# A first modulation whose bias comes by channels, with three weight tiles on a second queue

## The chip, the cores and the metric

The kernel runs on one core of one Trainium2 chip. The metric is the device time of one execution in microseconds; the kernel before takes 1773.36 us (median of 3 runs). TensorE multiplies matrices, VectorE (DVE in the profile), ScalarE (ACT) and GpSimd (POOL) work on vectors, and SyncE (SP) issues the transfers between the chip's main memory and the core's on-chip memory. Sixteen DMA engines carry them.

## The reference, cut to what matters

One layer of a diffusion backbone over 512 latent tokens and 256 context tokens, 1024 channels wide. Two condition vectors (for the latent and for the context tokens) give six modulation vectors each, by one product with `w_mod` (1024 x 6144) and a bias `b_mod`. The first two of the six shift and scale the first norm:

```python
cond, cond_c = silu(c), silu(c_ctx)
mod = cond @ w_mod + b_mod            # six vectors of 1024; mod_c likewise
h = rmsnorm(x, norm1) * (1 + mod[1]) + mod[0]
cols = h @ w_in                       # input projection, feeds three mixers
...                                   # convolution, recurrence, grid attention, merge, residual
...                                   # second norm, router, 16 experts, residual
```

Everything after the first norm needs `mod[0]` and `mod[1]`; the other four vectors are needed later.

## The kernel before

The program is written out by hand in the order in which it shall run, and each engine takes its instructions in that order. It has a start, a first sub-layer (to about 760 us in the trace), the output projection with the router, and sixteen experts whose weights, 384 chunks of 1 MiB, pass through a ring of buffers; a chunk is loaded when the products with an older one have freed its buffer.

The start does two things side by side. *Tokens*: `load_x` loads each tile of 128 tokens as two pieces of 128 x 512 (2 KB a row, 256 KB a piece, tiles named `y`); `stats` (L248, ScalarE) sums their squares, `scales` (L252 to L257) normalises them, TensorE transposes them (L266), and VectorE and ScalarE copy the transposes to `xT` (L268). *First modulation*: the condition vectors `cc` are put through silu into `cs`; the columns 0 to 2047 of `w_mod` come as eight tiles `wm0[k]` of 128 x 2048 (1 MiB each, k0 to k7, in the buffers A, A, C and wm, two tiles in each), and `mod_mm` (L303) multiplies each with `cs` as four products of 512 columns in four groups of 32 rows, summed over k in one PSUM bank. TensorE has the transposes ahead of these products in its order.

Afterwards the bias is added (`mod_rows`, L307), four transposes bring the rows to channels on partitions (`mod_cols`, L313), a copy takes the two columns that matter out of PSUM (L315), and L368 makes the scale `ga1`. From then on `modulate` (L381, L382) gives the projection's operands, while casts (L353) and differences (L354) split the first projection weights `W` into two parts.

The bias of the rows is read from main memory by `bias_row`: its source pattern is four rows of 512 numbers, each read 32 times, into 128 x 512.

```python
SP.dma_start(out=t, in_=bass.AP(tensor=a["b_mod"].tensor, offset=a["b_mod"].offset + g * 2048,
                                ap=[[512, 4], [0, 32], [1, 512]]))
```

It is called three times: for the first modulation and, later, for the two other groups of columns, whose weights are loaded in slabs (L468). All transfers are issued by SP in the order of the program: `cc`, eight token pieces, the small operands `vecs` (39 columns), k0 to k5, the bias rows, k6, k7, the first two items of the projection's weights, the context tokens.

## Time and profile before

| | us |
|---|---|
| time, median of 3 runs | 1773.36 (1773.16 to 1774.51) |
| profiled execution, first to last instruction | 1770.6 |
| of it, until the first group of projection products ends | 54.3 |
| of it, the first sub-layer after that, to the output projection | 54.3 to 760 |
| of it, experts' products and weights at full rate | 838 to 1770.6 |

Of the profiled execution the profile has the span alone, which begins with the first instruction and ends with the last; the times of the runs also hold what lies around it, so the median stands 2.8 us above the span. Over the span TensorE is busy for 94%, VectorE 32%, ScalarE 21%. Such shares are averages over stages with different limits, and what a change in the first 40 us is worth has to be read from that stage.

### The profile page before, as it was taken

The page shows a single profiled execution, that of the slowest core. Times are in us where ns is not written, and L with a number is a line of the kernel's source. Part 1 is how long each engine was busy: PE and PEld are TensorE (multiplying, and loading weights), DVE is VectorE, ACT ScalarE, POOL GpSimd, SP SyncE. Part 2 cuts the span into 40 slices and gives each one's busy share as a digit, 9 for nine tenths or more (in the row PEclk, how much of TensorE's full clock was granted, in tenths as well). Part 3 has the DMA queues.
Part 4 walks back from the last instruction along what each step waited for, and adds up shares of the span by engine and source line. Part 5 has one row for each costly group of instructions (what it writes and reads, how often), then busy time and mean ns, then how long its engine had stood idle before and what let it go on. Part 6 is the DMA issues. An engine that isn't in the chain of part 4 may idle for free.

```text
span 1770.6 us, 20476 instructions
## 1 busy us (share of the span) xinstructions
PE 1667.7 (94%) x8382; PEld 949.9 (54%) x8382; DVE 572.1 (32%) x1135; ACT 367.7 (21%) x759; POOL 79.0 (4%) x150
## 2 busy tenths in 40 slices
PE   4999999999999999999999999998998998989988
PEld 2767888777777888896343343342432422424322
DVE  3518776435553443334011211121121121202111
ACT  4414445333334332223000010000000100000000
POOL 0214330000000000000000000000000000000000
PEclk8999999999999999999999999999999999999999
DMA  9860111111111233366999999999999999999997
GB/s 343 283 227 25 50 51 67 48 66 66 66 60 42 92 132 109 137 233 238 401 420 420 420 420 421 420 421 420 420 420 421 420 420 421 420 420 420 421 420 299
DMA packets 131690, 487.77 MB, mean 275 GB/s; under 512 B 8973, under 2 KB 12557, under 8 KB 125709
## 3 DMA queue, kind: packets, MB, share of 16 engines
q1 hardware_dynamic: 131596, 486.47, 69.2%
q8 instruction: 66, 1.08, 0.2%
q14 instruction: 28, 0.22, 0.0%
HBM read 484.34 MB, written 2.10 MB: 275 GB/s over the span
## 4 chain that ended last, share of the span: by engine, by line
PE 73%; DMA 11%; DVE 5%; ACT 1%; issue 1%; SPq 0%; DVEq 0%; ACTq 0%
PE pj L1343 19%; PE pj L440 19%; PE acc L1368 9%; PE hg L1397 5%; PE pj L985 4%; PE hg L1311 3%; PE pj L1175 2%; DMA B<-in_w_down_dram 2%; DMA D<-in_w_down_dram 2%; DMA W<-in_w_up_dram 2%; DMA B<-in_w_up_dram 2%; PE acc L910 2%; DVE acc L1400 2%; PE hg L879 1%; DMA A<-in_w_down_dram 1%; PE tp L896 1%
## 5 line engine op out<-in xcount | busy, mean ns | idle before, releaser
L440 PE MATMUL pj<-A,W 128*128 128x512 f32 x1536 | 400.8, 402 | 2.9 <-ACT W L353 1.9
L440 PEld LDWEIGHTS pj<-A,W 128*128 128x128 f32 x1536 | 276.4, 190 | 73.6 <-issue 20.1
L354 DVE TENSOR_TENSOR W<-W 128x512 fp32r<-128x512 f32 (+1 forms) x184 | 121.4, 686 | 155.4 <-ACT W L353 155.2
L1350 DVE TENSOR_TENSOR s<-s,pj 128x512 f32<-128x512 f32 x32 | 22.0, 688 | 453.7 <-PE pj L1343 367.0
L1343 PE MATMUL pj<-W,xe 128*64 128x512 f32 x688 | 156.5, 599 | 7.8 <-DMA W<-in_w_up_dram 4.4
L1348 ACT ACTIVATE s<-pj 128x512 f32<-128x512 f32 x32 | 19.1, 597 | 567.8 <-PE pj L1343 567.8
L1343 PE MATMUL pj<-A,xe 128*64 128x512 f32 x512 | 118.0, 605 | 5.2 <-DMA A<-in_w_gate_dram 4.2
L1397 PE MATMUL hg<-ye,oht 64*128 64x512 f32 x240 | 100.4, 683 | 16.5 <-DVE acc L1400 16.5
L1343 PEld LDWEIGHTS pj<-W,xe 128*64 128x64 f32 x688 | 47.4, 138 | 110.5 <-issue 86.4
L1343 PE MATMUL pj<-B,xe 128*64 128x512 f32 x432 | 98.5, 596 | 6.6 <-DMA B<-in_w_up_dram 4.4
L353 ACT CAST W<-W 128x512 fp32r<-128x512 f32 (+1 forms) x184 | 103.3, 600 | 0.0
L1400 DVE TENSOR_TENSOR acc<-acc,hg 128x512 f32<-128x512 f32 x120 | 77.7, 684 | 37.1 <-PE hg L1397 37.1
L1343 PEld LDWEIGHTS pj<-A,xe 128*64 128x64 f32 x512 | 35.2, 139 | 81.8 <-issue 66.3
L1397 PEld LDWEIGHTS hg<-ye,oht 64*128 64x128 f32 x240 | 32.7, 193 | 81.8 <-DVE acc L1400 69.6
L1389 DVE TENSOR_TENSOR ye<-mod,acc 64x512 f32<-64x512 f32 x30 | 20.6, 686 | 172.2 <-PE acc L1368 171.7
L1368 PE MATMUL acc<-W,at 128*64 128x512 f32 x320 | 71.7, 595 | 2.1 <-DMA W<-in_w_down_dram 2.1
L1343 PEld LDWEIGHTS pj<-B,xe 128*64 128x64 f32 x432 | 29.5, 137 | 70.0 <-issue 52.9
L1358 ACT COPY at<-tp 128x512 f32<-128x512 f32 x32 | 18.8, 586 | 219.1 <-PE tp L1356 218.6
L440 PEld LDWEIGHTS pj<-C,W 128*128 128x128 f32 x384 | 59.2, 190 | 9.2 <-ACT y L612 0.8
L440 PE MATMUL pj<-C,W 128*128 128x256 f32 x384 | 61.8, 283 | 0.0
L1311 PEld LDWEIGHTS hg<-ot,xn 128*128 128x128 f32 x512 | 57.9, 192 | 2.7 <-issue 2.7
L1311 PE MATMUL hg<-ot,xn 128*128 128x128 f32 x512 | 59.1, 276 | 0.2 <-DVE ot L1297 0.2
(289 smaller groups left out, 1875.1 us busy)
## 6 DMA issues: line engine op xcount, KB each, us to landing
W<-in_w_gate_dram SPq DMA_DIRECT2D x44, 1024.0 KB, 18.1
W<-in_w_up_dram SPq DMA_DIRECT2D x42, 1024.0 KB, 17.7
W<-in_w_down_dram SPq DMA_DIRECT2D x40, 1024.0 KB, 18.0
W<-in_w_in_dram SPq DMA_DIRECT2D x34, 1024.0 KB, 4.8
A<-in_w_gate_dram SPq DMA_DIRECT2D x34, 1024.0 KB, 18.1
B<-in_w_up_dram SPq DMA_DIRECT2D x34, 1024.0 KB, 17.5
B<-in_w_down_dram SPq DMA_DIRECT2D x31, 1024.0 KB, 18.1
A<-in_w_up_dram SPq DMA_DIRECT2D x30, 1024.0 KB, 17.9
```

The costliest lines, as they stand in the source:

```text
L353: S.copy(hi[:, sl], raws[n][:, sl])
L354: V.tensor_tensor(lo[:, sl], raws[n][:, sl], hi[:, sl].bitcast(F32), op=ALU.subtract)
L440: PE.matmul(dst, w[wi][:, k, 128 * b:128 * b + 128], src[xi][:, k], start=(k == 0 and p == 0), stop=(k == KT - 1 and p == 2))
L910: PE.matmul(po[r, 128 * cb:128 * cb + 128], vs[c][:, hc], pT[:, 128 * c:128 * c + 128], start=(c == 0), stop=(c == 3))
L985: PE.matmul(st["p"], wb[wi][:, 4 * br + k], yv[br][k][xi], start=(k == 0 and p == 0), stop=(k == 3 and p == 2))
L1175: PE.matmul(st["p"][:, 256 * u:256 * u + 256], mm[k][mi][:, ts], w[wi][:, k], start=(k == 0 and p == 0), stop=(k == KT - 1 and p == 2))
L1311: PE.matmul(px[:, 128 * k:128 * k + 128], xn[:, i, 128 * kk:128 * kk + 128], ot[:, 128 * i:128 * i + 128], start=(i == 0), stop=(i == 3))
L1343: PE.matmul(pg[64 * u:64 * u + 64], xp[:, kk, 64 * (e % 2):64 * (e % 2) + 64], wt[:, k, 512 * u:512 * u + 512], start=(kk == 0), stop=(kk ...
L1350: V.tensor_tensor(est["s", j], est["s", j], pg, op=ALU.mult)
L1368: PE.matmul(est["y"][64 * u:64 * u + 64], lhs, wt[:, k, 512 * u:512 * u + 512], start=(kk == 0), stop=(kk == 15))
L1397: PE.matmul(pc, oht[64 * u:64 * u + 64, 128 * i:128 * i + 128], ye[64 * u:64 * u + 64], start=True, stop=True)
L1400: V.tensor_tensor(av, av, pc, op=ALU.add)
```

## The change

The bias of the first modulation is not loaded as rows any more. Its 2048 numbers stand in sixteen more columns of `vecs`, by channels, and are added in the operation that copies the transposed columns out of PSUM. The PSUM bank with the products' sums is copied by two engines, one half of the columns each. The first three weight tiles are issued by ScalarE's queue, in the program ahead of the tokens; the other five follow the tokens and `vecs` on SP's queue. The other two bias rows stay as they were.

```diff
     out["vecs"] = np.concatenate([kt(a["norm1"][0]), kt(a["norm2"][0]), lb, a["hg_norm"][0][:, None],
                                   np.tile(a["na_q_norm"][0], 2)[:, None], np.tile(a["na_k_norm"][0], 2)[:, None],
-                                  cw], axis=1)
+                                  cw, kt(a["b_mod"][0][0:1024]), kt(a["b_mod"][0][1024:2048])], axis=1)
...
     cc = small([128, KT, 2], "cc")
-    SP.dma_start(out=cc, in_=a["cc"])
-    for i in range(4):
-        load_x(i)
-    vecs = small([128, 39], "vecs")
-    SP.dma_start(out=vecs, in_=a["vecs"])
+    vecs = small([128, 55], "vecs")
...
-    def load_mod0(k):
+    def load_mod0(k, eng):
...
-        SP.dma_start(out=wm, in_=a["w_mod"][k * 128:(k + 1) * 128, 0:2048])
+        eng.dma_start(out=wm, in_=a["w_mod"][k * 128:(k + 1) * 128, 0:2048])
...
     wmt = []
-    for k in range(8):
-        if k == 6:
-            brow0 = bias_row(0)
-        load_mod0(k)
+    SP.dma_start(out=cc, in_=a["cc"])
+    for k in range(3):
+        load_mod0(k, S)
+    for i in range(4):
+        load_x(i)
+    SP.dma_start(out=vecs, in_=a["vecs"])
+    for k in range(3, 8):
+        load_mod0(k, SP)
...
-    def mod_cols(g, mr):
+    def mod_cols(g, mr, bias=None):
...
-        V.tensor_copy(mt, pt.rearrange("p (i j x) -> p j i x", i=4, j=4)[:, :, :, 0:2])
+        pv = pt.rearrange("p (i j x) -> p j i x", i=4, j=4)[:, :, :, 0:2]
+        if bias is None:
+            V.tensor_copy(mt, pv)
+        else:
+            V.tensor_tensor(mt, pv, bias.rearrange("p (j i) -> p j i", j=4).unsqueeze(3).broadcast_to([128, 4, 4, 2]),
+                            op=ALU.add)
...
-    mod0 = mod_cols(0, mod_rows(pm, brow0))
+    mr0 = g512()
+    V.tensor_copy(mr0[:, 0:256], pm[:, 0:256])
+    S.copy(mr0[:, 256:512], pm[:, 256:512])
+    mod0 = mod_cols(0, mr0, vecs[:, 39:55])
```

The line numbers move by a few: L303 stays, L307 and L315 become L372 and L319 for the first modulation, L338 becomes L343.

The start of SP's queue before. A name in brackets is the counter for which a transfer waits; there are eight of them, given out in turn, so that a transfer waits for the one eight places ahead of it.

```order
L190 DMA cc<-in_cc_dram 128x16
L187 DMA y<-in_x_dram 128x512 x7
L187 DMA y<-in_x_dram 128x512 [waits DMAHW0_49]
L194 DMA vecs<-in_vecs_dram 128x39 [waits DMAHW1_49]
L215 DMA A<-in_w_mod_dram 128x2048 [waits DMAHW2_49]
L215 DMA A<-in_w_mod_dram 128x2048 [waits DMAHW3_49]
...
L215 DMA C<-in_w_mod_dram 128x2048 [waits DMAHW7_49]
L203 DMA g<-in_b_mod_dram 128x1x512 [waits DMAHW0_49]
L215 DMA wm<-in_w_mod_dram 128x2048 [waits DMAHW1_49]
L215 DMA wm<-in_w_mod_dram 128x2048 [waits DMAHW2_49]
L338 DMA W<-in_w_in_dram 128x2048 [waits DMAHW3_49]
```

The same place of the change:

```order
L215 DMA cc<-in_cc_dram 128x16
L187 DMA y<-in_x_dram 128x512 x5
L187 DMA y<-in_x_dram 128x512 [waits DMAHW0_49]
L187 DMA y<-in_x_dram 128x512 [waits DMAHW1_49]
L187 DMA y<-in_x_dram 128x512 [waits DMAHW2_49]
L220 DMA vecs<-in_vecs_dram 128x55 [waits DMAHW4_49]
L211 DMA A<-in_w_mod_dram 128x2048 [waits DMAHW5_49]
L211 DMA C<-in_w_mod_dram 128x2048 [waits DMAHW6_49]
L211 DMA C<-in_w_mod_dram 128x2048 [waits DMAHW7_49]
L211 DMA wm<-in_w_mod_dram 128x2048 [waits DMAHW0_49]
L211 DMA wm<-in_w_mod_dram 128x2048 [waits DMAHW1_49]
L343 DMA W<-in_w_in_dram 128x2048 [waits DMAHW2_49]
```

The bias rows and three weight tiles are gone from this queue, and the last three token pieces have waits of their own; DMAHW0 there belongs to the first weight tile on ScalarE's queue.

The start of ScalarE's instructions before (squares of the tokens are `g,ssq<-y`):

```order
L229 ACT_TABLE_LOAD
L229 ACTIVATE csg<-cc 128x16 [waits DMAHW0_49]
L248 ACTIVATE g,ssq<-y 128x512 [waits DMAHW1_49]
L248 ACTIVATE g,ssq<-y 128x512 [waits DMAHW2_49]
L248 ACTIVATE g,ssq<-y 128x512 [waits DMAHW3_49]
```

The same place of the change:

```order
L211 DMA A<-in_w_mod_dram 128x2048 x2
L211 DMA A<-in_w_mod_dram 128x2048 [waits DMAHW3_49]
L229 ACT_TABLE_LOAD
L229 ACTIVATE csg<-cc 128x16 [waits DMAHW1_49]
L248 ACTIVATE g,ssq<-y 128x512 [waits DMAHW2_49]
L248 ACTIVATE g,ssq<-y 128x512
L248 ACTIVATE g,ssq<-y 128x512 [waits DMAHW4_49]
```

Three transfers now stand ahead of the table load, and the third of them waits for DMAHW3, the counter of the second token piece.

## Rows read from the trace of the kernel before

**Rows 1.** Head of the page, and packets of all transfers (counts under a size are cumulative).

```profile
span 1770.6 us, 20476 instructions
...
DMA packets 131690, 487.77 MB, mean 275 GB/s; under 512 B 8973, under 2 KB 12557, under 8 KB 125709
```

**Rows 2.** Stretches: busy time by engine, granted clock, DMA engines' share, rate.

```profile
core 0: us, PE busy (x) PEld busy (x) DVE busy (x) ACT busy (x) POOL busy (x), PEclk, DMA share, GB/s
4.00:10.00 6.00, 0.00 (x0) 0.00 (x0) 0.00 (x0) 4.31 (x13) 0.00 (x0) 1.00 0.93 308
14.00:25.00 11.00, 10.29 (x72) 5.86 (x72) 6.23 (x18) 3.84 (x6) 0.00 (x0) 1.00 1.02 427
25.00:29.50 4.50, 1.06 (x8) 0.16 (x8) 0.00 (x0) 0.00 (x0) 0.00 (x0) 0.82 1.02 268
29.50:36.00 6.50, 3.49 (x16) 0.40 (x16) 0.00 (x0) 0.00 (x0) 0.00 (x0) 0.50 1.01 421
54.33:760.00 705.67, 694.76 (x3752) 552.26 (x3752) 354.75 (x719) 256.80 (x540) 71.21 (x139) 1.00 0.27 93
64.00:67.50 3.50, 3.50 (x32) 3.50 (x31) 0.45 (x2) 1.95 (x4) 0.39 (x1) 1.00 1.04 235
838.00:1770.60 932.60, 868.89 (x3955) 317.04 (x3954) 159.63 (x292) 60.51 (x109) 0.00 (x0) 0.99 1.01 413
```

**Rows 3.** Timeline of TensorE: start, us, then what, with the idle time before.

```profile
14.02 5.86 PE L266 MATMUL pj<-ident,y 128*128 128x128 f32 x32 [14.02 <-DVE y L257]
19.80 3.64 PE L303 MATMUL acc<-A,g 128*32 128x512 f32 x32
23.26 1.04 PE L303 MATMUL acc<-C,g 128*32 128x512 f32 x8
25.42 1.06 PE L303 MATMUL acc<-C,g 128*32 128x512 f32 x8 [1.11 <-DMA C<-in_w_mod_dram]
31.98 1.94 PE L303 MATMUL acc<-wm,g 128*32 128x512 f32 x8 [5.50 <-DMA wm<-in_w_mod_dram]
34.45 1.94 PE L303 MATMUL acc<-wm,g 128*32 128x512 f32 x8 [0.53 <-DMA wm<-in_w_mod_dram]
37.20 1.12 PE L313 MATMUL tp<-ident,g 128*128 128x128 f32 x4 [0.81 <-DVE g L307]
...
102.77 0.60 PE L313 MATMUL tp<-ident,g 128*128 128x128 f32 x4
```

**Rows 4.** Timeline of VectorE around the first modulation's end.

```profile
36.45 0.69 DVE L307 TENSOR_TENSOR g<-acc,g 128x512 f32<-128x512 f32 x1 [13.46 <-PE acc L303]
38.35 0.19 DVE L315 COPY modT<-tp 128x32 f32<-128x32 f32 x1 [1.21 <-PE tp L313]
38.58 0.17 DVE L368 SCALAR_TENSOR_TENSOR ga<-modT,vecs 128x16 f32<-128x16 f32 x1
```

**Rows 5.** Timeline of ScalarE: table load, last squares, first cast of weights.

```profile
0.73 1.28 ACT L229 ACT_TABLE_LOAD   x1 [0.73 <-PEq L1464]
...
10.31 0.63 ACT L248 ACTIVATE g<-y 128x512 f32<-128x512 f32 x1
10.85 0.19 ACT L248 ACTIVATION_READ_ACCUMULATOR g<-y 128x1 f32 x1
...
39.56 0.60 ACT L353 CAST W<-W 128x512 fp32r<-128x512 f32 x1
```

**Rows 6.** Waits of SP's queue, 0 to 50 and 54 to 75 us.

```profile
SPq L187 <- DMA g<-in_b_mod_dram: 4.0, 1, 4.0
...
SPq L468 <- DMA g<-in_b_mod_dram: 4.2, 1, 4.2
```

**Rows 7.** Waits of TensorE, 54 to 760 us: total, times, longest.

```profile
PE hg L711 <- DVE g L712: 4.7, 3, 3.1
PE pj L529 <- DVE W L354: 2.0, 1, 2.0
```

**Rows 8.** Groups by form, 0 to 300 us: copies out of PSUM.

```profile
L268 DVE COPY g<-pj 128x512 f32<-128x512 f32 x4 | 2.8, 691 | 0.7 <-PE pj L266 0.7
L757 DVE COPY g<-hg 128x128 f32<-128x128 f32 x6 | 1.7, 290 | 2.4 <-PE hg L754 2.4
L613 ACT ACTIVATE g<-pj 128x256 f32<-128x256 f32 x8 | 3.0, 379 | 1.4 <-PE pj L440 1.4
```

## The prediction

> **What bounds the kernel now.** I read the span and the packet counts first [rows 1], then stretches of the span with the granted clock and the DMA rate [rows 2], then the timelines of TensorE, VectorE and ScalarE over the first 40 us [rows 3 to 5], and last who waits for whom [rows 6, 7]. After 54 us the kernel is a long train: TensorE is busy in 694.76 of the 705.67 us up to 760, with the DMA engines at 0.27 [rows 2], and what it waits for there is VectorE, 4.7 us the longest item, with no transfer in the list [rows 7]. From 838 us the expert weights stream at 413 GB/s with the engines at 1.01 of their time [rows 2]; each of those loads is issued when a product frees its buffer, so this stream starts when the train before it arrives. Nothing in either part has a clock of its own. I therefore take a shift of the first part's end as a shift of the kernel's end, one for one.

> The first part is where TensorE stands still. The transposes of the normalised tokens run from 14.02, and at 19.80 the products with the first modulation's eight weight tiles (k0 to k7) begin [rows 3]. Four need 3.64 us and k4 follows at once, but k5 waits for its tile until 25.42, k6 until 31.98 and k7 until 34.45 [rows 3]. The last product ends at 36.39, and the evacuation, four transposes and two small operations carry it to 38.75 [rows 3, 4]. So the weights set the end of this part, and the tokens, ready at 19.80, have slack. The steps between tiles are unequal: k6 to k7 takes 2.47 us, which is 1 MiB at 425 GB/s, and k5 to k6 takes 6.56. Between k5 and k6 stands one transfer, the bias rows of 256 KB.

> **The bias rows (removed).** In 25 to 29.5 us the engines are busy 1.02 of the time and move 268 GB/s, against 427 before and 421 after [rows 2]. A second bias row, near 66 us, shows the same dip, 235 GB/s at a share of 1.04 [rows 2]. SP, each of whose transfers waits in the program for the one eight places before it, waits 4.0 us for the first and 4.2 us for the second [rows 6]. By bytes it would cost 0.262 MB at 427 GB/s, 0.6 us. By the rate lost in the dip it costs (427 - 268) x 4.5 / 427 = 1.7 us more, 2.3 in all. By the tile that waits it costs 6.56 - 2.47 = 4.1 us. A tile has landed when the slowest of its engines is done, so I take the last: 4.1 us, with 0.6 kept as the other end. k7 then lands at 34.45 - 4.1 = 30.3.

> **The bias by channels (added).** Sixteen more columns in the small vector load are 8 KB, under 0.05 us at the same rate. The addition moves into the copy of the transposed columns, 32 elements, 0.19 us before [rows 4]; with a second operand I take 0.20.

> **The second queue (moved).** Three weight tiles, 3.15 MB, go to ScalarE's queue beside the tokens. While the tokens load, the engines are at 0.93 and move 308 GB/s [rows 2]; filling that up to 427 for 6 us is worth (427 - 308) x 6 / 427 = 1.7 us of all that comes behind. So the weights' bounds are 30.3 (nothing filled) and 28.6 (all). One more product at the full clock, 1.04 us as k4's [rows 3], ends that path at 31.4 or 29.7.

> [...]

> **The tokens' path is what becomes late.** The tokens (2.10 MB) now share the engines with 3.15 MB of weights. By the order of the program the sixth token transfer waits for the first weight tile, and ScalarE's third weight transfer waits for the second token transfer, with the table load and the sums of squares queued behind it. From the landing of the last token piece: 0.8 us for its squares (0.63 and the read of the sum, [rows 5]). In before these end at 11.04 and the products start at 19.80 [rows 3, 5], so 8.76 us later, of ScalarE, VectorE and TensorE work that doesn't change. Then eight tiles at 3.46 / 4 = 0.865 us (19.80 to 23.26) and a tail of 0.2 are 7.1 us, with no waits. Products end = landing + 0.8 + 8.76 + 7.1 = landing + 16.7.

> The landing: bytes flow from about 2.5 us. With equal shares 4.2 MB go before it; at 427 GB/s that is 9.8 us, landing 12.3; at a middle rate of 370, 11.3 us, landing 13.8. With the weights wholly ahead, 3.15 MB at 427 and 2.10 MB at 308 are 7.4 + 6.8 = 14.2 us, landing 16.7. Weights move in longer packets than tokens: of the kernel's 131690 packets 125709 are under 8 KB, 12557 of these under 2 KB [rows 1], and a row of a tile is 8 KB against 2 KB for a token piece, so if the engines alternate by packets, weights win. I therefore take 15.8, nearer that end. Products end at 15.8 + 16.7 = 32.5, later than the weights' 31.4: the bound passes from the weights to the tokens, and part of the 4.1 us is not collected. Against 36.39 this is 3.9 us. ScalarE's own queue doesn't bind: if the second token piece lands near 7, then third issue 0.4, table load 1.28, and eight squares at 0.72 end near 14.8, before the last piece is through.

> **The tail.** Before, from 36.39 to 38.75: VectorE adds over 512 columns in 0.69, the transposes take 1.12, the copy 0.19, the next step 0.17, and gaps [rows 3, 4]. Now two halves of 256 columns are copied by two engines at once. No such VectorE copy is in the trace; it lies between 0.29 for 128 columns and 0.69 for 512 [rows 8], by a straight line 0.42; ScalarE reads 256 columns of PSUM in 0.38 [rows 8]. That saves 0.27. [...] The same four transposes take 0.60 us at 102.77, in a stretch at the full clock [rows 3]. With the products now back to back to the end, the clock should hold: 0.52 more, or nothing if it falls. Tail 0.27 to 0.79; I take 0.7.

> **Sum.** 3.9 + 0.7 = 4.6 us. The first weights of the input projection, needed by a cast at 39.56 [rows 5], land one tile (2.47 us) behind k7, at 32.8 or earlier; the cast now wants them near 35, so they hide. The profiled span 1770.6 becomes 1766.0; the median lies 2.8 us above the span (launch and end), so 1773.4 - 4.6 = 1768.8.

> **Rivals.**
> A: tokens come early (equal shares, idle filled). Landing 12.3 gives products at 29.0, and the weights' 29.7 binds: 36.39 - 29.7 + 0.79 = 7.5 us, 1765.9; with the middle rate 30.5, so 6.7 us, 1766.7. For it: tokens left 7% of the engines idle. Against it: the packet sizes and the cross waits. Chance 0.16.
> B: weights wholly ahead: landing 16.7, products 33.4, 3.0 + 0.7 = 3.7 us, 1769.7; with some rate lost on top, 2 to 3.5 us. [...] I give 0.14 to gains of 2 to 3.5 us; around 3.7 it is the near edge of the forecast.
> C: the bias rows cost their bytes alone and k6 was late for something else: weights at 34.45 - 0.6 + 1.04 = 34.9 bind; 1.5 + 0.7 = 2.2 us or less, down to nothing, 1771.2 to 1773.4. Against it speaks the second dip. Chance 0.09.
> D: gained here and lost behind, in the VectorE-bound stretch at 150 us [rows 7], by a clock step that falls otherwise: within 0.2%. Chance 0.05.
> E, the other side: the two queues hinder each other, as the bias rows hindered all. At 235 GB/s, the lowest stretch seen [rows 2], 5.24 MB need 22.3 us: landing 24.8, products 41.5, 5.1 us late less the tail's 0.7, 1777.8. The point: below about 290 GB/s the gain is gone. Chance 0.06.

> **How the numbers follow.** Forecast (gains of 3.6 to 5.6 us) 0.50. About 3.5 us, 0.2%, is what a measurement of this kernel tells from no change. Faster by more: forecast and A, 0.66. Within: B, C, D, 0.28. Slower: E, 0.06. The range 1766.0 to 1771.6 holds the forecast, nearly all of A, and B, and cuts most of C, D and all of E.

> **What would show it.** Right: no 268 GB/s dip before 30 us; k5 to k7 about 2.5 us apart or not waited for; the products starting near 25 instead of 19.80 and running without idle, at the full clock; four transposes near 0.6 us. Wrong: a product that still waits for k7 (weights bind, A or C), token sums that end after 20 us (E), or a modulation ready 4 to 5 us earlier with an end that isn't.

## The result and the profile after

The changed kernel takes 1793.93 us (median of 4 runs, 1792.23 to 1794.25) against 1773.26 us (4 runs, 1771.73 to 1774.51): a ratio of 1.012, interval 1.0106 to 1.0134. It is 20.7 us slower, where 4.6 us faster was predicted. The profiled execution spans 1791.9 us, against 1770.6 [rows 1]. Two executions of the runs below, at a lower granted clock (1912.85 us at 0.84 in k1_before_224_bytes, 2376.19 us at 0.67 in k2_before_d_at_64), are left out of all medians and ratios.

The first 40 us don't show that. Here is TensorE's timeline of the kernel after: start in us, busy us, the instructions, and in brackets how long the engine had stood idle and for what.

```profile
19.68 6.00 PE L266 MATMUL pj<-ident,y 128*128 128x128 f32 x32 [19.68 <-DVE y L257]
25.61 3.64 PE L303 MATMUL acc<-A,g 128*32 128x512 f32 x32
29.07 1.90 PE L303 MATMUL acc<-C,g 128*32 128x512 f32 x16
30.79 1.90 PE L303 MATMUL acc<-wm,g 128*32 128x512 f32 x16
33.24 0.84 PE L313 MATMUL tp<-ident,g 128*128 128x128 f32 x4 [0.55 <-DVE g L372]
35.92 0.50 PE L448 MATMUL pj<-A,W 128*128 128x512 f32 x1 [1.85 <-ACT W L358]
```

The products of the modulation begin at 25.61 instead of 19.80 and run to 32.69 with no wait between them; before, the last of them waited for its weights until 34.45 [rows 3]. The first product of the input projection comes at 35.92, 4.3 us earlier than before, whose row is this:

```profile
40.21 0.79 PE L440 MATMUL pj<-A,W 128*128 128x512 f32 x1 [1.90 <-ACT W L353]
```

The loss is told by the same kind of windows as before, after's here: stretch in us, its length, then busy us and count of PE, PEld, DVE, ACT and POOL, the granted clock, the DMA share, GB/s.

```profile
25.00:29.50 4.50, 4.50 (x42) 1.62 (x44) 1.60 (x8) 2.38 (x4) 0.00 (x0) 1.00 1.02 422
29.50:36.00 6.50, 4.10 (x37) 1.26 (x29) 1.43 (x5) 1.82 (x4) 0.00 (x0) 1.00 1.01 398
54.00:760.00 706.00, 697.09 (x3767) 554.38 (x3766) 350.83 (x712) 253.08 (x534) 70.96 (x139) 1.00 0.27 95
838.00:1791.90 953.90, 870.33 (x3944) 312.89 (x3940) 158.95 (x291) 59.99 (x108) 0.00 (x0) 0.99 1.01 403
1000.00:1600.00 600.00, 545.17 (x2476) 197.50 (x2474) 100.65 (x185) 38.05 (x69) 0.00 (x0) 0.99 1.03 409
```

The dip of 268 GB/s at 25 us is gone (422), the clock in the tail is 1.00 instead of 0.50, and the long middle is as it was. But from 838 us on, where the experts' weights stream, 403 GB/s flow where 413 did [rows 2], at the same share of 1.01. The ends of the stage dilute the rate; in the middle of it, 1000 to 1600 us, the kernel before reads:

```profile
1000.00:1600.00 600.00, 557.98 (x2554) 204.45 (x2550) 101.95 (x187) 38.85 (x71) 0.00 (x0) 0.99 1.02 420
```

420 GB/s before, 409 after, with the DMA engines full in both: 2.6% less. The trace also holds the time of every packet. Of the packets of 4 KB that start between 1000 and 1600 us, 99.6% take 159 ns in the kernel before and 14% in the kernel after; the mean rises from 159.2 to 163.6 ns, 2.7%. So each transfer is slower in itself. The first expert product starts at 830.54 before and at 828.09 after, as these two rows say, of before and of after:

```profile
830.54 1.94 PE L1343 MATMUL pj<-A,xe 128*64 128x512 f32 x8
```

```profile
828.09 1.94 PE L1351 MATMUL pj<-A,xe 128*64 128x512 f32 x8
```

So the experts' stage lasts 1770.6 - 830.54 = 940.1 us before and 1791.9 - 828.09 = 963.8 after, 23.7 more; 940.1 x 420 / 409 = 965.4 is what the rate alone makes of it. Of the 4.3 us gained at the start 2.5 are still there at 828 us (though kernels with the old start differ there by some 2 us, 828.40 in g1 and 830.63 in k2), and the stage behind, whose code the change doesn't touch, loses nearly ten times as much.

What the change does to that stage is not in its code but in where its buffers lie. The small vector tile `vecs` grows from 39 to 55 columns of 4 bytes; with rounding it takes 224 bytes of each partition instead of 160. Tiles are placed one behind the other, so all behind it move by 64 bytes, the ring into which the experts' weights are loaded too. In the built programs (an address is not in the profile) eight of the ring's nine buffers, A twice, B twice, C, and W three times, start at multiples of 256 bytes before (A at 43520) and 64 past one after (43584). The ninth, D, starts 224 past one in both. That was the theory to be tested. One rival was the second queue, left open to the end and hindering the first; the other was main memory, where the wider `vecs` operand could have moved the weights.

### The profile page after: what moved, and what is told of

Its sections match the earlier page's. It is cut to its first block, busy times and chain, and to the rows that moved or that the text cites. A ratio compares the mean times of both kernels' runs of the same rounds, so it can differ in the third digit from the quotient of the medians.

```text
span 1791.9 us, 20472 instructions
## 1 busy us (share of the span) xinstructions
PE 1671.0 (93%) x8382; PEld 948.1 (53%) x8382; DVE 571.4 (32%) x1135; ACT 367.3 (21%) x760; POOL 78.8 (4%) x150
## 3 DMA queue, kind: packets, MB, share of 16 engines
q10 hardware_dynamic: 432, 3.15, 0.5%
## 4 chain that ended last, share of the span: by engine, by line
PE 64%; DMA 21%; DVE 5%; ACT 1%; issue 1%; SPq 0%; DVEq 0%; ACTq 0%
PE pj L448 19%; PE pj L1351 15%; PE acc L1376 5%; PE hg L1405 5%; DMA A<-in_w_up_dram 4%; PE pj L993 4%; PE hg L1319 3%; DMA W<-in_w_up_dram 3%; DMA B<-in_w_up_dram 3%; PE pj L1183 2%; DMA B<-in_w_down_dram 2%; DMA A<-in_w_gate_dram 2%; DMA W<-in_w_gate_dram 2%; DMA B<-in_w_gate_dram 2%; DMA A<-in_w_down_dram 2%; PE acc L918 2%
## 5 line engine op out<-in xcount | busy, mean ns | idle before, releaser
L1405 PE MATMUL hg<-ye,oht 64*128 64x512 f32 x240 | 98.5, 670 | 16.7 <-DVE acc L1408 16.7
L1351 PE MATMUL pj<-C,xe 128*64 128x512 f32 x256 | 59.4, 604 | 2.5 <-DMA C<-in_w_gate_dram 2.5
L1376 PE MATMUL acc<-B,at 128*64 128x512 f32 x240 | 55.6, 598 | 5.6 <-DMA B<-in_w_down_dram 5.6
```

Source lines behind the costliest of these rows:

```text
L1351: PE.matmul(pg[64 * u:64 * u + 64], xp[:, kk, 64 * (e % 2):64 * (e % 2) + 64], wt[:, k, 512 * u:512 * u + 512], start=(kk == 0), stop=(kk ...
L1376: PE.matmul(est["y"][64 * u:64 * u + 64], lhs, wt[:, k, 512 * u:512 * u + 512], start=(kk == 0), stop=(kk == 15))
L1405: PE.matmul(pc, oht[64 * u:64 * u + 64, 128 * i:128 * i + 128], ye[64 * u:64 * u + 64], start=True, stop=True)
```

## The experiments

All medians stand against runs of the kernel before in the same batch on the same chip (1771.76 to 1771.98 us). "Rate" is that of 1000 to 1600 us.

| run | median us | ratio (95% interval) | rate GB/s |
|---|---|---|---|
| e1_queue_old_addresses | 1769.22 | 0.9986 (0.9978 to 0.9995) | 420 |
| e2_before_64_bytes | 1798.03 | 1.0144 (1.0128 to 1.0160) | 409 |
| e3_change_one_queue | 1793.52 | 1.0117 (1.0101 to 1.0132) | 409 |
| e4_before_second_queue | 1770.29 | 0.9991 (0.9981 to 1.0002) | 420 |
| f1_before_32_bytes | 1796.05 | 1.0134 (1.0119 to 1.0150) | 409 |
| f2_before_128_bytes | 1795.86 | 1.0134 (1.0120 to 1.0148) | 409 |
| k1_before_224_bytes | 1797.36 | 1.0138 (1.0122 to 1.0153) | 409 |
| f3_before_256_bytes | 1771.79 | 1.0000 (0.9991 to 1.0009) | 420 |
| g1_before_ninth_buffer | 1774.05 | 1.0009 (1.0000 to 1.0018) | 420 |
| k2_before_d_at_64 | 1774.12 | 1.0011 (1.0002 to 1.0020) | 420 |
| h2_before_w_odd | 1783.59 | 1.0060 (1.0046 to 1.0074) | 418 |
| h3_before_w_b_odd | 1786.96 | 1.0084 (1.0071 to 1.0096) | 415 |
| m1_change_ring_at_256 | 1768.85 | 0.9982 (0.9973 to 0.9991) | 420 |
| m2_one_queue_ring_at_256 | 1767.71 | 0.9974 (0.9964 to 0.9984) | 420 |

### Addresses or queue

**The whole change, with the old addresses.** `vecs` keeps 39 columns, and the sixteen of the bias go by a transfer of their own into a buffer that exists already.

```diff
-    vecs = small([128, 55], "vecs")
+    vecs = small([128, 39], "vecs")
+    bcol = g512()[:, 0:16]
-    SP.dma_start(out=vecs, in_=a["vecs"])
+    SP.dma_start(out=vecs, in_=a["vecs"][:, 0:39])
+    SP.dma_start(out=bcol, in_=a["vecs"][:, 39:55])
-    mod0 = mod_cols(0, mr0, vecs[:, 39:55])
+    mod0 = mod_cols(0, mr0, bcol)
```

> The change, but vecs keeps its 39 columns and the sixteen bias columns go by a transfer of their own into a buffer of the g group, so that every later on-chip buffer lies where it lay before the change; main memory and the second queue stay as in the change. The start was 4.2 us earlier in the change (34.55 against 38.79 us for the first modulated operand). Address theory (the 64 bytes by which the ring's buffers moved slow every transfer into them): the experts' stream is back at 420 GB/s, the time about 1769, 4 us below before. Queue theory (a second queue, once opened, slows every later transfer): 409 GB/s and about 1793. Main memory theory (the wider vecs operand moves the weights in main memory): 409 GB/s and about 1793.

**The kernel before, with 64 unused bytes.** Nothing of the change but the shift.

```diff
     vecs = small([128, 39], "vecs")
+    pad = small([128, 16], "pad")
+    V.memset(pad, 0.0)
```

> The kernel before with 64 unused bytes behind vecs, nothing else (and one memset of them). Address theory: all ring buffers but the last start 64 bytes later, 409 GB/s in the experts' stage, about 1797 (1773.3 and 24 to 25 us). Queue theory and main memory theory: no change, 1773.

**The change on one queue.** All eight weight tiles behind the tokens on SP's queue; `vecs` stays wide.

```diff
-    for k in range(3):
-        load_mod0(k, S)
...
-    for k in range(3, 8):
+    for k in range(8):
         load_mod0(k, SP)
```

> The change with all eight weight tiles on SP's queue behind the tokens, no transfer on ScalarE's queue; the bias stays in the 55 columns of vecs. Address theory and main memory theory: 409 GB/s, 1793 to 1796. Queue theory: 420 GB/s, 1769 to 1771. In the start, whatever the theory: k7 is reached about 4 us earlier than in before (bias rows gone), without the second queue's part.

**The second queue alone.** The kernel before, bias rows kept, with the first three tiles on ScalarE's queue.

```diff
-    SP.dma_start(out=cc, in_=a["cc"])
-    for i in range(4):
-        load_x(i)
...
-    SP.dma_start(out=vecs, in_=a["vecs"])
...
-        SP.dma_start(out=wm, in_=a["w_mod"][k * 128:(k + 1) * 128, 0:2048])
+        eng.dma_start(out=wm, in_=a["w_mod"][k * 128:(k + 1) * 128, 0:2048])
...
-    for k in range(8):
+    SP.dma_start(out=cc, in_=a["cc"])
+    for k in range(3):
+        load_mod0(k, S)
+    for i in range(4):
+        load_x(i)
+    SP.dma_start(out=vecs, in_=a["vecs"])
+    for k in range(3, 8):
         if k == 6:
             brow0 = bias_row(0)
-        load_mod0(k)
+        load_mod0(k, SP)
```

> The kernel before with the second queue alone: the first three weight tiles on ScalarE's queue, the bias rows still loaded between k5 and k6, vecs with 39 columns. Address theory and main memory theory: 420 GB/s, 1771 to 1774. Queue theory: 409 GB/s, 1795 to 1798.

The four runs part the theories. Whatever moves the ring by 64 bytes is 1.2 to 1.4% slower, with one queue (e3) as with two, and with nothing else changed at all (e2). Whatever leaves the ring in place has its 420 GB/s, with two queues (e1, e4) as with one. Main memory is out as well: e2 leaves it as it was and is slow, e1 has the wider operand and is not. The windows of e2 and e1 from 1000 to 1600 us, each kernel's own:

```profile
1000.00:1600.00 600.00, 546.07 (x2486) 197.69 (x2482) 100.55 (x185) 38.05 (x69) 0.00 (x0) 0.99 1.02 409
```

```profile
1000.00:1600.00 600.00, 557.64 (x2551) 205.06 (x2548) 103.58 (x190) 38.65 (x70) 0.00 (x0) 0.99 1.03 420
```

The share is 1.02 and 1.03, so the engines are no less busy in the slow one; each packet takes longer (163.5 ns in e2, 159.2 in e1, counted as above), and TensorE, which goes at the pace of these loads, gets through 2486 instructions instead of 2551. e2 shows the loss without any other part of the change, e1 that the rest of the change gains 2.5 us (0.9 to 3.9 by the interval).

### Which shifts cost

The same unused tile in the kernel before with 8, 32, 56 and 64 columns, that is 32, 128, 224 and 256 bytes:

```diff
     vecs = small([128, 39], "vecs")
+    pad = small([128, 64], "pad")
+    V.memset(pad, 0.0)
```

> The kernel before with 32 unused bytes behind vecs (ring buffers A, B, C, W, until now at multiples of 512 bytes, start 32 behind one). If any start off a 64-byte multiple costs more than one off 512: more than the 64 bytes' 409 GB/s loses, below 405 and over 1800. If every odd start costs the same: 409 GB/s, 1794 to 1798.

> The kernel before with 128 unused bytes behind vecs (ring buffers start 128 behind a multiple of 512). If only 256- or 512-byte starts are free: 409 GB/s, 1794 to 1798. If 128-byte starts are free: 420 GB/s, 1772.

> The kernel before with 256 unused bytes behind vecs (ring buffers start 256 behind a multiple of 512). If 256-byte starts are free: 420 GB/s, 1772. If only 512-byte starts are: 409 GB/s, 1794 to 1798.

> The kernel before with 224 unused bytes behind vecs: eight ring buffers start 224 behind a multiple of 256, as D always did. If 224 is a cheap start (D's alignment then had nothing to give): 420 GB/s, 1772 to 1774. If every start off 256 costs the same and D is special by its place: 409 GB/s, 1794 to 1798.

A shift by 32, 64, 128 or 224 bytes costs 1.3 to 1.4%, all alike within their intervals; one by 256 costs nothing. So it is no matter of distance, nor of multiples of 512 (f3's buffers lie 256 past one): a buffer starts on a multiple of 256 bytes or it doesn't.

### Which buffers cost

If each buffer off a multiple of 256 pays its share, two more runs follow: the ninth, D, which is off in the kernel before, should gain when it is put on one, and a ring of which only a part is off should pay that part. For D an unused tile of 120 columns ahead of it puts it on a multiple of 512 (g1), one of 104 columns puts it 64 past a multiple of 256 (k2):

```diff
+    wpad = wk.tile([128, 120], F32, name="wpad", bufs=1)
+    V.memset(wpad, 0.0)
```

> The kernel before with the ninth ring buffer (D), which started 480 bytes behind a multiple of 512, moved to a multiple of 512 by 480 unused bytes; the other eight stay. Going from eight good starts to none cost 25 us, so one buffer costs about 3 us: 1769, if each transfer pays by its own destination. If what counts is another thing that the 64 bytes moved (the small tiles, the token buffers), nothing: 1772.

> The kernel before with D alone moved from 224 to 64 bytes behind a multiple of 256 (416 unused bytes beside it). If 224 is cheap and 64 is not: about 3 us later, 1775. If D never pays: 1772.

For the part, W's three buffers move into a pool of their own behind 64 unused bytes (h3: W and, behind it, B are off); 192 more bytes behind that pool put B back (h2: W alone).

```diff
+    gap_p = ctx.enter_context(tc.tile_pool(name="gap", bufs=1, side="left"))
+    gap_t = gap_p.tile([128, 16], F32, name="gap_t")
+    nc.vector.memset(gap_t, 0.0)
+    strw = ctx.enter_context(tc.tile_pool(name="streamw", bufs=1, side="left", reuse_waits="tile"))
...
-        return str_.tile([128, 4096], dt, tag=tag, name=tag, bufs={"A": 2, "W": 3, "C": 1}[tag])
+        return (strw if tag == "W" else str_).tile([128, 4096], dt, tag=tag, name=tag, bufs={"A": 2, "W": 3, "C": 1}[tag])
```

> The kernel before with only the three W buffers 64 bytes off (64 unused bytes ahead of them, 192 behind, so that B starts at a multiple of 256 again): with D four of nine ring buffers start off a 256-byte multiple. If every transfer pays by its own destination: 3/8 of the 24 us, 409 to 416 GB/s, about 1781. [...]

> The kernel before with the W and B buffers 64 bytes off (64 unused bytes ahead of W): with D six of nine ring buffers start off a 256-byte multiple. Own destination alone: 5/8 of the 24 us, about 1787. [...]

The more buffers are off, the more is lost. By span less the start of the first expert product, the stage takes 948.3 us in h2 (1781.6 - 833.35) and 951.8 in h3 (1784.2 - 832.44), 8.2 and 11.7 more than before's 940.1, with three and five buffers off; with all eight it was 23.7. That is 2.7, 2.3 and 3.0 us a buffer, where kernels with an undisturbed ring differ from each other in this stage by some 3.5 us (939.8 in e4, 943.3 in e1). That the loss is in proportion is not shown: the rate in the middle fell by 2 and 5 of the 11 GB/s, where three and five eighths would be 4 and 7. If every transfer paid by its own destination, the expectations asked for 1781 in h2 and 1787 in h3; 1783.59 and 1786.96 were measured. If a few buffers off cost nothing, h2 would have stayed near the 1771.84 of the kernel before, which it didn't. Inside h2 the rate goes up and down with the buffer that is being filled, as its TensorE timeline shows, where one product group of the stream after the other waits for 1 MiB of weights:

```profile
1220.33 1.94 PE L1375 MATMUL acc<-B,at 128*64 128x512 f32 x8 [0.57 <-DMA B<-in_w_down_dram]
1222.81 1.94 PE L1350 MATMUL pj<-B,xe 128*64 128x512 f32 x8 [0.55 <-DMA B<-in_w_gate_dram]
1225.28 1.94 PE L1350 MATMUL pj<-B,xe 128*64 128x512 f32 x8 [0.53 <-DMA B<-in_w_gate_dram]
1227.85 1.94 PE L1350 MATMUL pj<-W,xe 128*64 128x512 f32 x8 [0.63 <-DMA W<-in_w_gate_dram]
1230.40 1.94 PE L1350 MATMUL pj<-W,xe 128*64 128x512 f32 x8 [0.62 <-DMA W<-in_w_gate_dram]
1232.96 1.94 PE L1350 MATMUL pj<-W,xe 128*64 128x512 f32 x8 [0.62 <-DMA W<-in_w_up_dram]
```

Pieces for B, which is on a multiple, come 2.47 to 2.48 us apart, pieces for W, which is not, 2.55 to 2.57 (2.51 for the last of these six, not shown): 3 to 4% within one run, a few us from each other. It is not W itself that is slow: in the kernel before the same six pieces for W come 2.46 to 2.54 apart, and in the kernel after, where both are off, B's and W's alike 2.55 to 2.57 where TensorE does nothing but wait for them, save the last of W's six, 3.49 behind the fifth. The windows of h2 over ten us each say the same in GB/s, the first mostly B's, the second W's alone:

```profile
1220.00:1230.00 10.00, 7.75 (x32) 1.94 (x32) 1.37 (x2) 0.00 (x0) 0.00 (x0) 1.00 1.02 419
1230.00:1240.00 10.00, 7.72 (x32) 1.94 (x32) 0.00 (x0) 0.60 (x1) 0.00 (x0) 1.00 1.03 410
```

D was a miss: with it on the multiple nothing is gained (1.0009, where 3 us or 0.9983 was expected), and 64 bytes past one it is no different (1.0011), at 420 GB/s both times. The packets say the same: D takes one load in nine, yet in the kernel before, with D 224 bytes past, only 0.4% of the packets take longer than 159 ns. Why this one buffer is exempt the runs don't tell. h2 and h3 also reach the experts 2 to 3 us later than before; kernels alike differ there by almost as much (828.40 in g1, 830.63 in k2), and it was not followed.

### The change with the ring put back

192 unused bytes between the small tiles and the ring bring the 64 to 256, the rest of the change stays (m1); the same with all eight tiles on SP's queue, as in e3 (m2).

```diff
+    gap_p = ctx.enter_context(tc.tile_pool(name="gap", bufs=1, side="left"))
+    gap_t = gap_p.tile([128, 48], F32, name="gap_t")
+    nc.vector.memset(gap_t, 0.0)
```

> The change with 192 unused bytes between the small tiles and the ring, so that the ring's buffers start at multiples of 256 again; vecs has its 55 columns, and the small tiles and the experts' accumulator stay 64 bytes on. If the ring's starts are the whole of it: 420 GB/s, 1768 to 1770. If the small tiles or the accumulator count: nearer to 1794.

> The same with all eight weight tiles on SP's queue (no second queue): the start of the one-queue run was as early as the change's (36.00 against 35.92 us for the first projection product), so if the second queue adds nothing to the end either: as the change with the ring at 256, 1768 to 1770. If the second queue helps beyond the start: 1771 to 1772.

Both stream at 420 GB/s, with the small tiles still 64 bytes on, so it is the ring's place that counts. Both beat the kernel before: m1 by 1771.84 - 1768.85 = 3.0 us, m2 by 4.1, the lowest median here. Here is TensorE's timeline of m2, where only SP's queue loads:

```profile
19.92 3.64 PE L304 MATMUL acc<-A,g 128*32 128x512 f32 x32
...
25.15 1.07 PE L304 MATMUL acc<-C,g 128*32 128x512 f32 x8 [0.73 <-DMA C<-in_w_mod_dram]
...
27.63 1.55 PE L304 MATMUL acc<-wm,g 128*32 128x512 f32 x8 [1.42 <-DMA wm<-in_w_mod_dram]
...
30.11 1.93 PE L304 MATMUL acc<-wm,g 128*32 128x512 f32 x8 [0.93 <-DMA wm<-in_w_mod_dram]
...
35.55 0.79 PE L449 MATMUL pj<-A,W 128*128 128x512 f32 x1 [1.85 <-ACT W L359]
```

The tokens are ready at 19.92, as in the kernel before, and the weights bind, k5, k6 and k7 at even steps of 2.48 us. The first projection product comes at 35.55, m1's at 35.73 and after's at 35.92: with the bias rows gone it makes no difference whether the weights bind (one queue) or the tokens (two). The intervals of m1 and m2 overlap, so neither is shown to be ahead.

## Why the prediction was wrong

**The step that failed** is the one that priced the bias by channels: "Sixteen more columns in the small vector load are 8 KB, under 0.05 us". That counts the transfer, and says nothing of the tile that receives it. The tile's growth moved the ring off its multiples of 256 bytes, and that cost 23.7 us in the experts' stage (26 us in the median of e2, which has the shift alone); e1, m1 and m2, which have the rest of the change with the ring on the multiple, don't pay it. A second sentence failed with it: "Nothing in either part has a clock of its own", from which a shift of the start became a shift of the end, one for one. The stream has one: its rate. Rows 2 showed that the engines there are full (1.01) for 930 us and that TensorE has to keep to their pace; 1% of that is 9 us, twice what the whole start could give. I asked when that stream would begin, and not whether each of its transfers would be the same. None of the rivals A to E held this. E, the only one that forecast a loss, had another mechanism: two queues that hinder each other in the start, with products that end at 41.5. They ended at 32.69, and 386 GB/s flowed from 2.5 to 10 us and 418 from 14 to 25, so E didn't come; nor does a second queue slow the stream later, as e1 and e4 stand at 420 GB/s with ScalarE's queue in use. The loss that came is no partial success of E.

TensorE's waits in after's experts' stage (us in all, times, longest) say how the loss looks from the engine: there is no new wait to speak of, and the old ones for weight buffers are longer, 48.2 us in all where the kernel before has 28.7. Two of them:

```profile
PE pj L1351 <- DMA W<-in_w_up_dram: 5.9, 8, 1.6
...
PE acc L1376 <- DMA W<-in_w_down_dram: 5.5, 10, 0.9
```

In the kernel before the same two were 4.4 and 2.1:

```profile
PE pj L1343 <- DMA W<-in_w_up_dram: 4.4, 8, 0.6
...
PE acc L1368 <- DMA W<-in_w_down_dram: 2.1, 4, 0.7
```

**The bias rows: right.** 4.1 us was taken from the tile that waits, not the 0.6 of their bytes. The counters of landed transfers in the trace of the kernel before show how: the bias row's landing is counted in four late steps, from 28.91 to 29.72, where a weight tile's is counted in sixteen, and of the tile behind it, k6, twelve parts have landed by 29.30 and the last four from 31.38 to 31.94. Read as one count for each engine, four of the sixteen carried the row, and each tile behind it waited for those four: the products with k6 begin at 31.98 [rows 3], behind the last of its parts and not behind the twelfth. "The slowest of its engines" was the right measure. In e3, which has one queue and no bias rows, k5, k6 and k7 come 2.48 us apart, where k5 to k6 took 6.56 before:

```profile
26.29 1.07 PE L301 MATMUL acc<-C,g 128*32 128x512 f32 x8 [1.06 <-DMA C<-in_w_mod_dram]
...
28.77 1.94 PE L301 MATMUL acc<-wm,g 128*32 128x512 f32 x8 [1.42 <-DMA wm<-in_w_mod_dram]
...
31.25 1.51 PE L301 MATMUL acc<-wm,g 128*32 128x512 f32 x8 [0.54 <-DMA wm<-in_w_mod_dram]
```

**The second queue: right that the bound passes to the tokens, wrong about what holds them.** The products were forecast from near 25 to 32.5 and ran from 25.61 to 32.69. But "ScalarE's own queue doesn't bind" fell. ScalarE's timeline of after, where ACTq is its issuing of transfers:

```profile
0.73 9.53 ACTq L211 DMA_DIRECT2D A<-in_w_mod_dram  x3
10.29 1.28 ACT L229 ACT_TABLE_LOAD   x1 [10.29 <-DMA y<-in_x_dram]
11.71 0.61 ACT L248 ACTIVATE g<-y 128x512 f32<-128x512 f32 x1
...
15.99 0.61 ACT L248 ACTIVATE g<-y 128x512 f32<-128x512 f32 x1
16.52 0.19 ACT L248 ACTIVATION_READ_ACCUMULATOR g<-y 128x1 f32 x1
```

Its three transfers hold it for 9.53 us, since the third waits for the second token piece; then come the table load and eight sums of squares, back to back to 16.71. From the first of them on there is no wait for a token piece. These two rows, of ScalarE's timeline and of SyncE's, give the landings: the third weight transfer goes out when the second token piece has landed, and the transfer of `W` when the eighth has.

```profile
9.93 0.33 ACTq L211 DMA_DIRECT2D A<-in_w_mod_dram  x1
```

```profile
13.98 2.94 SPq L343 DMA_DIRECT2D W<-in_w_in_dram  x2
```

So the last piece had landed by 13.98, two microseconds before its squares began at 15.99; it was the engine that was late, held by its own queue. The forecast put the second piece at 7, and it landed just before 9.93. From there its own terms for ScalarE (0.4, 1.28 and eight times 0.72, which give 14.4 from 7, where 14.8 was written) make 17.4, later than the 16.6 that the landing gave for the end of the squares, and this path would have been seen to bind. The landing at 15.8 was a wrong term that by luck gave a similar number. B's landing, 16.7 with the weights wholly ahead, didn't come either; that the weights win if the engines alternate by packets was an inference of the prediction, and by what turns the engines serve two queues no run shows.

Where the stream is otherwise unbroken, the second queue brought the first projection product hardly forward: 36.00 in e3, with one queue, against 35.92 in after, with two. With the bias rows still there the second queue did give something: in e4 that product comes at 37.90 instead of 40.21, though the kernel's gain, 1.5 us, can't be told from none (0.9981 to 1.0002).

**The tail: right in sum, not in parts.** VectorE's timeline of after:

```profile
32.76 0.42 DVE L372 COPY g<-acc 128x256 f32<-128x256 f32 x1 [3.95 <-PE acc L303]
34.12 0.19 DVE L319 TENSOR_TENSOR modT<-tp,vecs 128x32 f32<-128x32 f32 x1 [0.94 <-PE tp L313]
```

The half copy takes the 0.42 of the straight line and the added operand costs nothing (0.19). ScalarE's half, however, starts only at 33.21, as VectorE's ends:

```profile
33.21 0.37 ACT L373 COPY g<-acc 128x256 f32<-128x256 f32 x1 [5.39 <-DVE g L372]
```

So the two halves didn't run at once. The four transposes take 0.84 instead of 0.60, at the full clock that was forecast; that they are longer because the halves come one behind the other is argued and not shown. That products back to back hold the clock, on which 0.52 of the tail was put, no run shows by itself: after's four transposes came 0.28 below the 1.12 of before, and in e2, where the products still wait (5.10 us for k6), they took 0.66. From the last product to the modulated operand ready for its first use it is 34.55 - 32.69 = 1.9 us, where 38.79 - 36.39 = 2.4 stood before: 0.5 gained for a forecast of 0.7. The two rows of that first use, of VectorE's timeline of before and of after:

```profile
38.79 0.55 DVE L381 TENSOR_SCALAR g<-g,ga,modT 128x512 f32<-128x512 f32 x1
```

```profile
34.55 0.55 DVE L389 TENSOR_SCALAR g<-g,ga,modT 128x512 f32<-128x512 f32 x1
```

**The sum.** At the operand it was 38.79 - 34.55 = 4.2 us of the 4.6 forecast. At the end, with the ring on multiples of 256 again, m1 keeps 3.0, in the gains of 2 to 3.5 that were B's, and m2 4.1, in the forecast's 3.6 to 5.6; by the intervals m1's gain is 1.6 to 4.8 us and m2's 2.8 to 6.4, so they don't part the two. What was argued of the start came out near its number, the landing by luck; what was taken for granted of the rest did not.

## What to carry to other kernels

A tile that grows moves the tiles placed behind it, here a ring by 64 bytes, so an edit in a kernel's start can change the transfers of its end, here from 420 to 409 GB/s: before pricing such an edit, list the start addresses of the buffers that a saturated stream fills, modulo 256 bytes, and pad the small tiles so that they stay. When a stage that was not touched is longer, compare its rate and its share first: here fewer GB/s at the same full share meant that each transfer cost more, and neither queues nor waits explained it. And an engine whose queue carries a transfer that waits for another's may not be free for its own work until that wait is over: here three transfers held ScalarE for 9.53 us.
